# Order of the split products within a k-tile of a two-layer encoder: both wide ones, then both narrow ones

## The chip, the cores and the metric

The kernel runs on one core of one Trainium2 chip. The metric is the device time of one execution in microseconds. Three runs of the kernel before gave 2452.22, 2452.59 and 2452.0 us, median 2452.22.

## The reference

The kernel computes a two-layer encoder trunk over one sequence of 256 tokens with 2048 features, in float32. Each layer is a token mixer and a gated MLP, both behind an RMSNorm and with a residual add:

```python
for layer in range(DEPTH):
    hn = rmsnorm(h, norm_mix_g[layer])
    if layer % 2 == 0:
        mix = mlstm_mixer(hn, ...)      # q, k, v, o, gates = hn @ w_in; two directions; y @ w_out
    else:
        mix = hgrn_mixer(hn, ...)       # q, i, g, f_f, f_b = hn @ w_in; two directions; y @ w_out
    h = h + mix
    h = h + conv_glu(rmsnorm(h, norm_ffn_g[layer]), ...)   # u = hn @ w_up; gelu(conv3(a)) * v; @ w_down
return rmsnorm(h, final_g)
```

D_FF is 5504, so an MLP's up-projection has 2 x 5504 columns. Some 110 million float32 weights are read once, and the work is mainly the products of these weights with 256 tokens.

## The kernel before

**Split products.** To get float32 accuracy from a faster matmul format, both operands are split into a high part (the value rounded to the format) and a low part (the rest). A product x w is taken as three terms: high x high, high x low and low x high. ACT makes the high part of a weight piece (`wh`, L146), DVE the low part (`wl`, L147). Activations are stored as `xt`, `ya`/`yb` or `g` tiles of 128 x 512: columns 0 to 255 hold the high part of 256 tokens, columns 256 to 511 the low part.

**Chunks.** All weights go through one stream of chunks (`stream`). A chunk is a block of output columns, contracted over `nk` k-tiles of 128 rows.

- Feature-major chunks (`fm`, 256 output columns) hold weights stationary: a k-tile is two halves `f` = 0, 1 of 128 columns, each with its own PSUM bank `ps[f]`. For each half L197 sends the whole activation tile through `wh` (512 columns: high and low part), and L198 sends its high part through `wl` (256 columns), adding to the first 256 columns of the same bank. So a k-tile is four matmuls with four different stationary operands.
- Token-major chunks (`tm`, 512 columns) hold activations stationary and send the weights: three products of 512 columns for each of two token blocks (L187 to L189).
- The chunk `first` is token-major with one more 128-column part, and the last chunk of the kernel (`last`, L176) is a feature-major chunk in which all products are 256 columns wide.

Feature-major are: q, k and the output projection of the first mixer; all up- and down-products of both MLPs (43 up-chunks of 16 k-tiles, 8 down-chunks of 22 and 8 of 21 k-tiles per layer); 24 chunks and the output projection of the second mixer.

**Supply.** SP loads raw pieces of 2048 columns into 3 buffers; each gives two `wh` and two `wl` pieces of 1024 columns (4 k-tiles of a feature-major chunk) in 4 buffers each, fetched three pieces ahead. PSUM gives four banks to chunks (`psm`, tag `mm`), so a chunk's two banks are used again two chunks later, and four to everything else (`psa`, tag `aux`).

**Side work.** The heads of both mixers run as generators (`Side`): `side.tick(dt)` behind each k-tile advances a count and emits the next step of any job that is due. The steps' matmuls are `S` (L426), `pn` (L440), `pz` (L468, L691), `pd` (L616, L657, L658) and `py` (L670).

**Order.** The program text gives an order, and the tile framework's scheduler, which works with a model of the engines' times, may move instructions within their dependencies. So the order on PE is that of the built program, not quite that of the loops. When a chunk's last k-tile is sent, `ch.done(ps)` emits its readers: ACT copies the low part out of PSUM (`b`, L209 or L310) and DVE adds (L210, or L311 and L312).

Of the kernel before, what the change touches and what calls it, by code (L numbers as in the profile page):

```python
# [15 lines left out]
P = 128  # L16
T = 256
# [36 lines left out]
def trunk_kernel(ctx, tc, xT, pp_d, cst_d, w_first, w_aq, w_ak, w_av, w_ao, w_aout,  # L54
                 w_bq, w_bv, w_bg, w_bout, w_up, w_down, out, mscr, stop=9):
    nc = tc.nc
    act, dve, pool, pe = nc.scalar, nc.vector, nc.gpsimd, nc.tensor
# [16 lines left out]
    def col(name, i):  # L74
        o = OFF[name] + i
        return pp[:, o:o + 1]
# [5 lines left out]
    class Side:  # L82
        def __init__(self):
            self.now, self.jobs = 0.0, []
# [25 lines left out]
    side = Side()  # L110


    class Chunk:
        def __init__(self, kind, src, nk, x, done, before=None, last=False):
            self.last = last
            self.kind, self.src, self.nk, self.x, self.done, self.before = kind, src, nk, x, done, before
            self.width = {"fm": 256, "tm": 512, "first": 512 + P}[kind]

    def split_weights(chunks):

        first = True
        for ch in chunks:
            total = ch.nk * ch.width
            cuts = [0]
            if ch.last and total % 1024:
                cuts.append(total % 1024)
            if first:
                cuts = [k * ch.width for k in FIRST]
            while cuts[-1] < total:
                cuts.append(min(total, cuts[-1] + 2048))  # L130
            step = ch.width if first else 1024
            for b0, b1 in zip(cuts, cuts[1:]):
                n = b1 - b0
                raw = wpool.tile([P, 2048], F32, tag="raw", bufs=RAW, name="raw")
                nc.sync.dma_start(raw[:, :n], ch.src[:, b0:b0 + n])
                if first:
                    k0, k1 = b0 // ch.width, b1 // ch.width
                    (nc.scalar if k0 < 2 else nc.sync).dma_start(hx[:, k0:k1], xT[:, k0:k1])
                    if k0 == 0:
                        nc.scalar.dma_start(pp[:, 0:KT], pp_d[:, 0:KT])  # L140
                for c0 in range(0, n, step):
                    m = min(step, n - c0)
                    wh = wpool.tile([P, 1024], F32R, tag="wh", bufs=WB, name="wh")
                    wl = wpool.tile([P, 1024], F32R, tag="wl", bufs=WB, name="wl")
                    r = raw[:, c0:c0 + m]
                    act.copy(wh[:, :m], r)  # L146
                    dve.tensor_tensor(wl[:, :m], r, wh[:, :m].bitcast(F32), ALU.subtract)  # L147
                    yield wh, wl, m // ch.width
            first = False

    def stream(chunks):
        pieces = split_weights(chunks)
        ready = []

        def fetch():
            p = next(pieces, None)
            if p is not None:
                ready.append(p)

        for _ in range(LOOK):  # L160
            fetch()
        for ch in chunks:
            if ch.before:
                ch.before()
            ps = [psm.tile([P, 512], F32, tag="mm", name="mm") for _ in range(3 if ch.kind == "first" else 2)]
            k = 0
            while k < ch.nk:
                fetch()
                wh, wl, n = ready.pop(0)
                if ch.last:  # L170
                    for f in range(2):
                        for kk in range(n):
                            x, c = ch.x(k + kk), kk * 256 + f * P
                            terms = ((wh, 0), (wl, 0), (wh, T))
                            for i, (w, o) in enumerate(terms):
                                pe.matmul(ps[f][:, 0:T], w[:, c:c + P], x[:, o:o + T], start=(k + kk == 0 and i == 0),  # L176
                                          stop=(k + kk == ch.nk - 1 and i == 2))
                    k += n
                    continue
                for kk in range(n):  # L180
                    x = ch.x(k)
                    st, sp = k == 0, k == ch.nk - 1
                    if ch.kind != "fm":
                        c = slice(kk * 512, (kk + 1) * 512)
                        for t in range(2):
                            xh, xl = x[:, t * P:(t + 1) * P], x[:, T + t * P:T + (t + 1) * P]
                            pe.matmul(ps[t], xh, wh[:, c], start=st, stop=False)  # L187
                            pe.matmul(ps[t], xh, wl[:, c], start=False, stop=False)  # L188
                            pe.matmul(ps[t], xl, wh[:, c], start=False, stop=sp)  # L189
                        if ch.kind == "first":  # L190
                            pe.matmul(ps[2], wh[:, 512:512 + P], x, start=st, stop=False)
                            pe.matmul(ps[2][:, 0:T], wl[:, 512:512 + P], x[:, 0:T], start=False, stop=sp)
                        side.tick(1.3)
                    else:
                        for f in range(len(ps)):
                            c = kk * ch.width + f * P
                            pe.matmul(ps[f], wh[:, c:c + P], x, start=st, stop=False)  # L197
                            pe.matmul(ps[f][:, 0:T], wl[:, c:c + P], x[:, 0:T], start=False, stop=sp)  # L198
                        side.tick(0.325 * len(ps))
                    k += 1  # L200
            ch.done(ps)

# [9 lines left out]
    def fm_scaled(ps, R, dst, scale=None):  # L212
        fm_sum(ps, dst)
        if scale is None:
            dve.tensor_tensor(dst, dst, R, ALU.mult)
        else:
            dve.scalar_tensor_tensor(dst, dst, scale, R, ALU.mult, ALU.mult)
# [101 lines left out]
    def slot(j, name, more=None):  # L319
        where = keep if j < KT else more  # L320
        return where.tile([P, 2 * T], F32R, tag=f"yt{j}", name=f"{name}{j}")
# [415 lines left out]
    def ffn(layer, norm, nxt):  # L737
        stack = ExitStack()
        box = {}
        chunks = []  # L740

        def begin():
            box["mp"] = stack.enter_context(tc.tile_pool(name="ff", bufs=1))

        def done_up(f, i, GT):
            def go(ps):
                mp, R = box["mp"], norm.R
                a = mp.tile([P, T], F32, tag="a", bufs=2, name="a")
                v = mp.tile([P, T], F32, tag="v", bufs=2, name="v")
                c = mp.tile([P, T], F32, tag="c", bufs=2, name="c")  # L750
                fm_scaled(ps[0], R, a)
                fm_scaled(ps[1], R, v)
                cw = [col("conv_w", (layer * 3 + w) * FT + f) for w in range(3)]
                dve.tensor_scalar(c, a, cw[1], col("conv_b", layer * FT + f), ALU.mult, ALU.add)
                dve.scalar_tensor_tensor(c[:, 1:T], a[:, 0:T - 1], cw[0], c[:, 1:T], ALU.mult, ALU.add)
                dve.scalar_tensor_tensor(c[:, 0:T - 1], a[:, 1:T], cw[2], c[:, 0:T - 1], ALU.mult, ALU.add)
                act.activation(c, c, AF.Gelu)
                dve.tensor_tensor(c, c, v, ALU.mult)
                g = slot(i, "g", mp)
                act.copy(g[:, 0:T], c)  # L760
                dve.tensor_tensor(g[:, T:2 * T], c, g[:, 0:T].bitcast(F32), ALU.subtract)
                GT.append(g)
            return go

        for part, (f0, nf) in enumerate(((0, FA), (FA, FB))):
            GT = []
            for i in range(nf):
                chunks.append(Chunk("fm", w_up[layer, f0 + i], KT, norm.x, done_up(f0 + i, i, GT),
                                    begin if f0 + i == 0 else None))
            chunks += project(lambda c: w_down[layer, c][:, f0 * 256:(f0 + nf) * 256], nf,  # L770
                              lambda k, GT=GT: GT[k], nxt if part else None)
        return chunks, stack.close
# [12 lines left out]
    if stop > 1:  # L785
        c, close0 = ffn(0, n1, n2)
        chunks += c
    if stop > 2:
        c = hgrn(n2, n3)
# [7 lines left out]
    if stop > 3:  # L797
        c, close1 = ffn(1, n3, nf)
        chunks += c
    stream(chunks)  # L800
    side.drain()
    if stop > 3:
# [90 lines left out]
```

## Time and profile before

| | us |
|---|---|
| median of three runs | 2452.22 |
| profiled execution, its own time | 2451.01 |
| its span, first to last instruction | 2449.2 |
| PE busy | 2432.1 |
| PE weight loads (beside PE) | 2108.3 |
| DVE busy | 1759.7 |
| ACT busy | 1221.2 |

| stage | from about, us |
|---|---|
| first mixer (q, k, v, o) | 7 |
| its output projection | 310 |
| first MLP | 400 |
| second mixer | 1116 |
| its output projection | 1626 |
| second MLP | 1719 |
| end of the last product | 2436 |

A matmul's duration in the profile reaches from its start to the modelled end of its pipeline, so successive matmuls overlap, and the time that one takes of PE is read from the distance of the starts. PE, PEld, DVE, ACT, POOL and SP are the tensor engine's matmuls and weight loads, the vector, the scalar, the gpsimd and the sync engine. PEq, PEldq and the like are an engine's queue.

### The profile page before, as it was taken

What the parts mean: (1) busy time and instruction counts of PE and PEld (TensorE: products, weight loads), DVE (VectorE), ACT (ScalarE), POOL (GpSimd) and SP (SyncE); (2) the same over time, 40 slices, a digit from 0 to 9 for tenths busy, and PEclk for the clock granted to TensorE, in tenths of its full rate; (3) what the DMA queues carried; (4) which work ended last, traced back from release to release, by engine and by line L of the source; (5) the groups of instructions that cost most, each with busy time, mean ns of one, the idle gap of its engine ahead of it and who ended that gap; (6) DMA issues with size and microseconds to landing.
All of it is one profiled execution on the core that took longest, in us unless ns stands there. A gap on an engine that the chain in (4) does not pass through costs nothing.

```text
span 2449.2 us, 36986 instructions
## 1 busy us (share of the span) xinstructions
PE 2432.1 (99%) x14462; PEld 2108.3 (86%) x14462; DVE 1759.7 (72%) x2943; ACT 1221.2 (50%) x1890; POOL 267.4 (11%) x325
## 2 busy tenths in 40 slices
PE   9999999999999999999999999999999999999998
PEld 7888888888888888888888888888888888888887
DVE  7766577777656777668888888888777755677754
ACT  6655455444444444445455555545544444444443
POOL 0100032000000000122222222224000000000022
PEclk9999999999999999999999999999999999999999
DMA  7654555555556555555544445445555555555553
GB/s 261 189 179 160 184 187 184 191 191 191 179 189 202 189 189 189 181 183 191 172 160 168 162 165 172 160 156 201 186 191 191 186 189 194 189 189 189 185 190 125
DMA packets 65920, 448.88 MB, mean 183 GB/s; under 512 B 7616, under 2 KB 8256, under 8 KB 15568
## 3 DMA queue, kind: packets, MB, share of 16 engines
q1 hardware_dynamic: 63936, 443.03, 54.2%
q0 software_dynamic: 800, 2.16, 0.6%
q8 instruction: 113, 1.85, 0.3%
q10 hardware_dynamic: 1008, 1.32, 0.2%
q14 instruction: 63, 0.52, 0.1%
HBM read 444.32 MB, written 2.16 MB: 182 GB/s over the span
## 4 chain that ended last, share of the span: by engine, by line
PE 98%; DVE 1%; ACT 0%; issue 0%; DMA 0%; SPq 0%; POOL 0%; DVEq 0%; POOLq 0%
PE mm L197 53%; PE mm L198 26%; PE mm L187 5%; PE mm L189 5%; PE mm L188 5%; PE pd L616 1%; PE pn L440 1%; PE mm L176 1%; PE py L670 1%; DVE wl L147 0%; PE S L426 0%; PE pd L657 0%; DMA raw<-in_w_first 0%; DVE QK L629 0%; PE pz L691 0%
## 5 line engine op out<-in xcount | busy, mean ns | idle before, releaser
L147 DVE TENSOR_TENSOR wl<-raw,wh 128x1024 fp32r<-128x1024 f32 (+1 forms) x864 | 1047.5, 1214 | 546.4 <-ACT wh L146 533.5
L197 PE MATMUL mm<-xt,wh 128*128 128x512 f32 x3776 | 1319.5, 395 | 0.0
L146 ACT CAST wh<-raw 128x1024 fp32r<-128x1024 f32 (+1 forms) x864 | 884.1, 1025 | 833.2 <-PE mm L197 481.5
L198 PE MATMUL mm<-xt,wl 128*128 128x256 f32 x3776 | 1049.9, 278 | 0.0
L197 PEld LDWEIGHTS mm<-xt,wh 128*128 128x128 f32 x3776 | 708.3, 188 | 164.3
L198 PEld LDWEIGHTS mm<-xt,wl 128*128 128x128 f32 x3776 | 710.1, 188 | 0.8
L197 PE MATMUL mm<-g,wh 128*128 128x512 f32 x1334 | 462.6, 394 | 0.0
L198 PE MATMUL mm<-g,wl 128*128 128x256 f32 x1334 | 369.5, 277 | 0.0
L197 PEld LDWEIGHTS mm<-g,wh 128*128 128x128 f32 x1334 | 250.1, 188 | 58.0
L198 PEld LDWEIGHTS mm<-g,wl 128*128 128x128 f32 x1334 | 250.5, 188 | 0.0
L187 PE MATMUL mm<-wh,xt 128*128 128x512 f32 x512 | 201.9, 398 | 3.1 <-ACT xt L204 2.5
L188 PE MATMUL mm<-wl,xt 128*128 128x512 f32 x512 | 201.5, 394 | 0.4 <-DVE wl L147 0.4
L189 PE MATMUL mm<-wh,xt 128*128 128x512 f32 x512 | 200.6, 393 | 0.0
L209 ACT COPY b<-mm 128x256 f32<-128x256 f32 x237 | 87.6, 370 | 172.2 <-PE mm L198 172.2
L243 POOL TENSOR_TENSOR acc<-hx 128x256 f32<-128x256 f32 x4 | 4.8, 1203 | 1238.3 <-DVE hx L312 1238.3
L187 PEld LDWEIGHTS mm<-wh,xt 128*128 128x128 f32 x512 | 95.7, 188 | 23.3 <-ACT xt L204 2.7
L189 PEld LDWEIGHTS mm<-wh,xt 128*128 128x128 f32 x512 | 96.5, 188 | 19.9
L188 PEld LDWEIGHTS mm<-wl,xt 128*128 128x128 f32 x512 | 96.5, 188 | 19.4 <-DVE wl L147 0.8
L197 PE MATMUL mm<-yb,wh 128*128 128x512 f32 x256 | 89.6, 396 | 0.0
L197 PE MATMUL mm<-ya,wh 128*128 128x512 f32 x256 | 89.1, 394 | 0.0
L246 POOL TENSOR_TENSOR sq<-hx 128x256 f32<-128x256 f32 x52 | 62.7, 1214 | 193.4 <-DVE hx L312 191.2
L210 DVE TENSOR_TENSOR a<-mm,b 128x256 f32<-128x256 f32 x86 | 36.5, 425 | 50.9 <-ACT b L209 50.7
(188 smaller groups left out, 1999.2 us busy)
## 6 DMA issues: line engine op xcount, KB each, us to landing
raw<-in_w_up SPq DMA_DIRECT2D x172, 1024.0 KB, 4.9
raw<-in_w_down SPq DMA_DIRECT2D x64, 1024.0 KB, 4.8
raw<-in_w_bq SPq DMA_DIRECT2D x48, 1024.0 KB, 4.9
raw<-in_w_ao SPq DMA_DIRECT2D x16, 1024.0 KB, 4.9
raw<-in_w_aout SPq DMA_DIRECT2D x16, 1024.0 KB, 4.9
raw<-in_w_bv SPq DMA_DIRECT2D x16, 1024.0 KB, 4.9
raw<-in_w_bg SPq DMA_DIRECT2D x16, 1024.0 KB, 4.9
raw<-in_w_bout SPq DMA_DIRECT2D x16, 1024.0 KB, 4.9
```

The source lines that it names most:

```text
L146: act.copy(wh[:, :m], r)
L147: dve.tensor_tensor(wl[:, :m], r, wh[:, :m].bitcast(F32), ALU.subtract)
L176: pe.matmul(ps[f][:, 0:T], w[:, c:c + P], x[:, o:o + T], start=(k + kk == 0 and i == 0), stop=(k + kk == ch.nk - 1 and i == 2))
L187: pe.matmul(ps[t], xh, wh[:, c], start=st, stop=False)
L188: pe.matmul(ps[t], xh, wl[:, c], start=False, stop=False)
L189: pe.matmul(ps[t], xl, wh[:, c], start=False, stop=sp)
L197: pe.matmul(ps[f], wh[:, c:c + P], x, start=st, stop=False)
L198: pe.matmul(ps[f][:, 0:T], wl[:, c:c + P], x[:, 0:T], start=False, stop=sp)
L209: act.copy(b, ps[:, T:2 * T])
L210: dve.tensor_tensor(dst, ps[:, 0:T], b, ALU.add)
L246: eng.tensor_tensor(s, hT[k], hT[k], ALU.mult)
L440: pe.matmul(pn[:, 0:258], w, v, start=(i == 0), stop=(i == len(parts) - 1))
```

## The change

In a feature-major k-tile, the two 512-column products of both halves are sent first and the two 256-column products after them; the call of `side.tick` stands between the two pairs. A chunk that is made with `plain=True` keeps the 512, 256, 512, 256 order, with `side.tick` behind all four. Only the up-products of the first layer's MLP are plain. Token-major chunks and the last chunk are as before. Lines below the edited loop move down by four.

```diff
     class Chunk:
-        def __init__(self, kind, src, nk, x, done, before=None, last=False):
-            self.last = last
+        def __init__(self, kind, src, nk, x, done, before=None, last=False, plain=False):
+            self.last, self.plain = last, plain
...
                     else:
-                        for f in range(len(ps)):
-                            c = kk * ch.width + f * P
-                            pe.matmul(ps[f], wh[:, c:c + P], x, start=st, stop=False)
-                            pe.matmul(ps[f][:, 0:T], wl[:, c:c + P], x[:, 0:T], start=False, stop=sp)
-                        side.tick(0.325 * len(ps))
+                        cs = [slice(kk * ch.width + f * P, kk * ch.width + (f + 1) * P) for f in range(2)]
+                        for f in range(2):
+                            pe.matmul(ps[f], wh[:, cs[f]], x, start=st, stop=False)
+                            if ch.plain:
+                                pe.matmul(ps[f][:, 0:T], wl[:, cs[f]], x[:, 0:T], start=False, stop=sp)
+                        side.tick(0.65)
+                        if not ch.plain:
+                            for f in range(2):
+                                pe.matmul(ps[f][:, 0:T], wl[:, cs[f]], x[:, 0:T], start=False, stop=sp)
                     k += 1
...
                 chunks.append(Chunk("fm", w_up[layer, f0 + i], KT, norm.x, done_up(f0 + i, i, GT),
-                                    begin if f0 + i == 0 else None))
+                                    begin if f0 + i == 0 else None, plain=layer == 0))
```

In the changed file the 512-column product is L197 in both forms; the 256-column product is L199 in a plain chunk and L203 in the others.

## The prediction

> **What bounds the kernel now.** I read the page first, then the waits, then the chain that ended last, in order of time. From the page:
>
> ```profile
> span 2449.2 us, 36986 instructions
> PE 2432.1 (99%) x14462; PEld 2108.3 (86%) x14462; DVE 1759.7 (72%) x2943; ACT 1221.2 (50%) x1890; POOL 267.4 (11%) x325
> PEclk9999999999999999999999999999999999999999
> PE 98%; DVE 1%; ACT 0%; issue 0%; DMA 0%; SPq 0%; POOL 0%; DVEq 0%; POOLq 0%
> L197 PE MATMUL mm<-xt,wh 128*128 128x512 f32 x3776 | 1319.5, 395 | 0.0
> L198 PE MATMUL mm<-xt,wl 128*128 128x256 f32 x3776 | 1049.9, 278 | 0.0
> L198 PEld LDWEIGHTS mm<-xt,wl 128*128 128x128 f32 x3776 | 710.1, 188 | 0.8
> ```
>
> PE carries 98% of the chain at full clock, and the two lines that the change reorders stand with no idle time. A busy PE may still lose time inside its stream, so the waits are not enough; they do say that little is left outside it (engine, line, who was waited for: total us, times, longest):
>
> ```profile
> PE pr L286 <- DVE dg L283: 1.4, 1, 1.4
> ...
> PE pd L616 <- DVE qm L608: 0.8, 1, 0.8
> ...
> PE pd L657 <- DVE QK L630: 0.4, 1, 0.4
> ```
>
> The durations of 395 and 278 ns overlap each other, so they are no price. The price is the step from one start to the next. The chain shows it (start, us taken, what); a row is the time until PE is handed to the next row:
>
> ```profile
> 49.42 0.23 PE mm L197
> 49.65 0.11 PE mm L198
> 49.76 0.23 PE mm L197
> 50.00 0.12 PE mm L198
> 50.11 0.46 PE mm L197 x2
> 50.57 0.24 PE mm L198 x2
> 50.81 0.23 PE mm L197
> ...
> 250.23 0.23 PE mm L187
> 250.45 0.23 PE mm L188
> 250.68 0.23 PE mm L189
> ...
> 2420.72 9.95 PE mm L176 x83
> ```
>
> Five readings. (1) An alternating k-tile (512, 256, 512, 256) runs from 49.42 to 50.11: 0.69 us. (2) The next k-tile was put by the scheduler as 512, 512, 256, 256, the order of the change, and runs from 50.11 to 50.81: 0.70 us, 693 ns start to start before rounding. (3) 512 behind 512, in the token-major chunks, steps 0.227 us in the trace, both where the next product adds to the same bank (L187 to L188) and where it goes to the other one (L189 to L187). (4) 256 behind 256, each with its own weights, steps 9.95/83 = 119.9 ns. (5) A clean stretch of the second layer's feed-forward:
>
> ```profile
> 1800.00:2400.00 600.00, 600.00 (x3464) 524.70 (x3463) 400.83 (x607) 285.84 (x407) 18.95 (x19) 1.00 0.57 190
> ```
>
> 600 us over 3464 matmuls is 173.2 ns each, four of them 692.8 ns. These fit one rule of this trace: 227 ns for a 512-column product and 120 ns for a 256-column one, whatever stands before it. 2 x 227 + 2 x 120 = 694 ns, against 692.8 measured in the alternating order.
>
> **The change, part by part.** The four feature-major groups of L197 have 3776 + 1334 + 256 + 256 = 5622 products, so 2811 k-tiles. The first layer's up-products, 43 chunks of 16, are 688 and keep their order; 2123 k-tiles change. Nothing is added or removed in arithmetic, loads, casts or DMAs.
>
> *Steps in the stream.* Before: two steps 512 to 256 and two 256 to 512. After: one each of 512 to 512, 512 to 256, 256 to 256 and 256 to 512. By the rule above both orders give 2 x 227 + 2 x 120, so 0 ns per k-tile. From the two directly timed k-tiles, (2) less (1) is 0.00 to 0.01 us; start to start, both are 693 ns. I take 0. The bounds come from mixing medians of unlike steps: 512 to 256 takes 233 ns, 256 to 512 115.5 ns on average, 512 to 512 227 ns, 256 to 256 120 ns. Replacing one 512-to-256 step and one 256-to-512 step by 512 to 512 and 256 to 256 gives 227 + 120 - 233 - 115.5 = -1.5 ns, or with 233 in place of 227 +4.5 ns: -3.2 to +9.6 us over 2123 k-tiles. These mix how starts are recorded with what they cost, so zero is the nearer row, because it is the same four instructions in the new order.
>
> *Weight loads.* Each product still has its load, and two loads per k-tile still have only a 256-column product to hide behind. What is new is that the two short ones follow each other. The load's row says 188 ns; if that bound a short product, the pair L203 to L203 would step 188 and not 120 ns, and the sum would be 2123 x 68 = +144 us. The 83 products of L176 are such a stream, each with its load, and step 119.9 ns. So I price it at 0. The Trainium skill (TensorE: Matmul & The Clock Gate, section LDWEIGHTS) gives a load as its columns over 1.2 GHz, so 107 ns for 128 of them: by that figure the load just fits under a 256-column product and this term is 0, where the 188 ns of the profile's row, taken as occupancy, makes it +144 us; the L176 stream agrees with the skill's figure and not with the row read that way.
>
> *Waits.* In the built program the PE queue holds 200 semaphore instructions in place of 56: ahead of L197, 130 of them wait for DVE where 4 did, because the second half's 512 product now comes ahead of the first wait for `wl` that used to cover the release of its PSUM bank. Queued behind such a wait on PE is the whole product stream. The bank was last read two chunks earlier; in the trace the last reader of a feature-major chunk ends at most 7.05 us after that chunk's last product and never less than 4.17 us before the chunk that takes the bank over. The reads of the first half start some 0.23 us later than now, because its 256 product moves behind the other half's 512; 4.17 - 0.23 leaves 3.9 us. So the waits are met when they are reached. The instruction itself:
>
> ```profile
> L197 PEldq EVENT_SEMAPHORE  x9: 51/51/51, 47.1 to 1971.6; - x9
> ```
>
> 144 x 51 ns = 7.3 us if all stood open. Four such stand within 0.4 us ahead of L197 at 652.9 us, and the steps around them stay 0.23 and 0.11 to 0.12 us. I take 0 and keep 7.3.
>
> *Weights and DMAs.* `wh` of a piece comes free some 0.12 us earlier, `wl` unchanged. ACT waits 481.5 us in all for L197 to release `wh`, DVE 533.5 us for ACT, PE 0.4 us once for `wl`; nothing on this path is late, and an earlier release starts casts earlier at no gain. SP's order of transfers is the same.
>
> *Side work.* `side.tick` moves from behind the pair of 256 products to between the 512s and the 256s; per k-tile it counts 0.65 as before. The built order shows where the head work lands: stretches of products are cut 111 times, not 120. One cut, the block at 1230 us: the nine steps ahead of it take 2.04 us, the nine behind 2.08 us, so 0.04 us beside the work itself; over the run the entry and settling come to about 0.1 us per cut. Nine fewer are -0.4 to -0.9 us; I take -0.6. The two waits of PE in the gated layer's start (0.8 and 0.4 us) belong to the second head's block; there DVE has the same 85 instructions to do first, and PE reaches it 0.2 us of products later, so about 1.0 of 1.2 us stays. The transposes of the finished heads stand 1 to 3 us earlier on PE, but their DVE work stands up to 5.5 us earlier too. Bounds: -1.2 (both waits go) to 3 x 1.2 = +3.6 us (the same waits come back in each of the other three groups of four heads).
>
> Sum: 0 + 0 + 0 - 0.6 = -0.6 us against the profiled execution's 2451.0 us (span 2449.2 and 1.8 around it): 2450.4. The median of the runs, 2452.2, lies 1.2 above that execution, so 2451.6.
>
> **The rivals.**
>
> *Banks, faster.* The step 512 to 256 goes to the same bank and takes 233 ns, 6 more than 512 to 512. If that is a wait for the bank just written, the new order, which changes bank at every product, loses it: 2 x 6 x 2123 = -25 us, 2426.6. Against: L187 to L188 stays in one bank and takes 227; 256 to 512 gives the 6 ns back (115.5 against 120). Chance 0.05.
>
> *Two short products in a row, slower.* The second load finds no slack saved up by a long product. From +9.6 us (the +4.5 ns above) up to +144 us (188 ns): 2461 to 2596; it decides from 4.9 us / 2123 = 2.3 ns per k-tile on. For it: a 120 ns step against a 188 ns load. Against: L176 and the k-tile at 50.11 us. Chance 0.04.
>
> *Semaphores, slower.* The 144 extra instructions are not run ahead of the products: +7.3 us, 2458.9; it passes 0.2% once two thirds are open. Against: the four at 652.9 us. Chance 0.04.
>
> *The order is undone.* The scheduler could have put the products back; the built program has 2099 steps 512 to 512 and 2090 steps 256 to 256 in place of 6 and 6, so this is out.
>
> **How the numbers follow.** No change within 0.2% (4.9 us, about what a measurement of this kernel can tell from none): 0.84. Faster: banks 0.05 and 0.02 for a luckier placement of side work, 0.07. Slower: 0.04 + 0.04 and 0.01 for side work, 0.09. The low end takes 1.2 and 0.9 us of side work off 2452.2, and 2 us more for the settling after cuts, which in all costs some 7 us in this trace: 2448. The high end adds the 3.6 us, with a further 1.2 for semaphores that stand open near the cuts: 2457. The rivals beyond hold less than 2 in 10.
>
> **What would show it.** Right: in a clean stretch of the second layer four products still take 693 ns; the chain reads 0.46 and 0.24 for the pairs; L197 and its 256-column partner show no idle time; the waits of PE are the same few. Wrong by banks: a k-tile of about 681 ns, everywhere outside the first layer's up-products. Wrong by loads: a pair of 256 products over 0.24 us. Wrong by semaphores: gaps only at starts of chunks. Wrong by side work: new waits of `pd`, `pz` or `S` for DVE between 20 and 310 us or 1116 and 1640 us.

## The result and the profile after

The changed kernel takes 2462.67 us (median of five runs, 2460.86 to 2462.79) against 2452.22: a ratio of 1.004, 95% interval 1.0028 to 1.0052. It is slower by about 10 us, where no change was forecast. The profiled execution took 2462.67 us with a span of 2460.9 us, 11.7 more than before. Two of the five executions took 2460.86 and 2461.18 us; the step between them and the others, some 1.7 us, is taken up with the waits below.

The page after, the lines that answer to those of before:

```profile
span 2460.9 us, 37193 instructions
PE 2440.9 (99%) x14462; PEld 2116.9 (86%) x14462; DVE 1758.4 (71%) x2943; ACT 1213.6 (49%) x1890; POOL 256.2 (10%) x325
PEclk9999999999999999999999999999999999999999
PE 95%; DVE 3%; issue 1%; ACT 0%; DMA 0%; SPq 0%; POOL 0%; DVEq 0%; POOLq 0%
L197 PE MATMUL mm<-xt,wh 128*128 128x512 f32 x3776 | 1237.4, 396 | 0.0
L203 PE MATMUL mm<-xt,wl 128*128 128x256 f32 x2400 | 478.4, 279 | 0.0
L199 PE MATMUL mm<-xt,wl 128*128 128x256 f32 x1376 | 386.2, 281 | 0.0
```

PE is busy 8.8 us longer with the same 14462 matmuls, and the three groups shown still have no idle time: most of the loss is inside the stream. DVE has a larger part of the chain, 3% for 1%. The waits of PE (engine, line, for whom: total us, times, longest):

```profile
PE pd L661 <- DVE QK L634: 3.1, 5, 0.7
...
PE mm L197 <- DVE hx L315: 1.8, 1, 1.8
```

The first was 0.4 us (and 0.8 us for another tile of the same block), the second was not there.

Where the 11.7 us went, by the starts of the chunks in the two traces: first product 0.35 us earlier; first mixer -1.1; its output projection +0.4; first MLP +5.7, of which its up-products, **whose order was not changed**, +4.5 and its down-products +1.15; second mixer -2.0; its output projection +5.55; second MLP +3.4; the end +0.2.

The same clean stretch as before (busy us and count of each engine; the second number on PE is the matmuls in 600 us), and a part of it in the chain:

```profile
1800.00:2400.00 600.00, 600.00 (x3448) 524.23 (x3447) 397.65 (x607) 280.90 (x405) 15.07 (x15) 1.00 0.57 188
```

```profile
2000.00 0.23 PE mm L203 x2
2000.23 0.47 PE mm L197 x2
2000.70 0.23 PE mm L203 x2
2000.93 0.46 PE mm L197 x2
```

3448 for 3464 products. Start to start, a grouped k-tile takes 696.7 ns on average (696.7 and 696.6 in turn), against 693.3: +3.3 ns, in every clean grouped chunk of this run. The pairs read as the prediction said, 0.46 or 0.47 and 0.23; one k-tile cannot show 3 ns at this resolution, the count over 600 us can.

The surprise is the other clean stretch, of up-products that alternate in both kernels. Kernel before, then after, 200 us in each half of the first layer's up-products:

```profile
430.00:630.00 200.00, 200.00 (x1156) 174.90 (x1156) 146.35 (x235) 98.64 (x145) 0.00 (x0) 1.00 0.57 190
780.00:980.00 200.00, 200.00 (x1156) 174.91 (x1155) 146.30 (x235) 98.60 (x144) 0.00 (x0) 1.00 0.57 190
```

```profile
430.00:630.00 200.00, 200.00 (x1156) 176.67 (x1155) 146.62 (x236) 98.97 (x145) 0.00 (x0) 1.00 0.57 190
780.00:980.00 200.00, 200.00 (x1134) 173.79 (x1133) 143.24 (x232) 97.11 (x141) 0.00 (x0) 1.00 0.56 185
```

The first half is equal, 1156 and 1156. In the second half the same order at the same full clock gives 1134 for 1156. Start to start, a k-tile takes 706.7 ns there, in all 21 chunks, where it takes 693.3 in the first half. So this order has two paces.

### The profile page after: what moved, and what is told of

It reads as the page before. It is cut to its first block, busy times and chain, and to the rows that moved or that the text cites. A ratio compares the mean times of both kernels' runs of the same rounds, so it can differ in the third digit from the quotient of the medians.

```text
span 2460.9 us, 37193 instructions
## 1 busy us (share of the span) xinstructions
PE 2440.9 (99%) x14462; PEld 2116.9 (86%) x14462; DVE 1758.4 (71%) x2943; ACT 1213.6 (49%) x1890; POOL 256.2 (10%) x325
## 4 chain that ended last, share of the span: by engine, by line
PE 95%; DVE 3%; issue 1%; ACT 0%; DMA 0%; SPq 0%; POOL 0%; DVEq 0%; POOLq 0%
PE mm L197 53%; PE mm L203 20%; PE mm L199 7%; PE mm L189 4%; PE mm L188 4%; PE mm L187 4%; DVE wl L147 1%; PE pd L620 1%; PE pn L444 1%; PE mm L176 1%; PE py L674 1%; DVE QK L633 0%; DVE QK L634 0%; DVE qm L612 0%; PE pd L661 0%
## 5 line engine op out<-in xcount | busy, mean ns | idle before, releaser
L197 PE MATMUL mm<-xt,wh 128*128 128x512 f32 x3776 | 1237.4, 396 | 0.0
L197 PEld LDWEIGHTS mm<-xt,wh 128*128 128x128 f32 x3776 | 626.4, 189 | 61.5
L203 PEld LDWEIGHTS mm<-xt,wl 128*128 128x128 f32 x2400 | 450.0, 188 | 102.4
L203 PE MATMUL mm<-xt,wl 128*128 128x256 f32 x2400 | 478.4, 279 | 0.0
L197 PE MATMUL mm<-g,wh 128*128 128x512 f32 x1334 | 419.0, 396 | 0.0
L199 PE MATMUL mm<-xt,wl 128*128 128x256 f32 x1376 | 386.2, 281 | 0.0
L203 PEld LDWEIGHTS mm<-g,wl 128*128 128x128 f32 x1334 | 251.0, 188 | 58.7
L203 PE MATMUL mm<-g,wl 128*128 128x256 f32 x1334 | 262.2, 278 | 0.0
L199 PEld LDWEIGHTS mm<-xt,wl 128*128 128x128 f32 x1376 | 260.3, 189 | 0.1
L197 PEld LDWEIGHTS mm<-g,wh 128*128 128x128 f32 x1334 | 203.4, 189 | 0.1
L213 ACT COPY b<-mm 128x256 f32<-128x256 f32 x237 | 79.7, 368 | 62.4 <-PE mm L199 62.4
L197 PE MATMUL mm<-yb,wh 128*128 128x512 f32 x256 | 83.4, 402 | 1.8 <-DVE hx L315 1.8
L197 PE MATMUL mm<-ya,wh 128*128 128x512 f32 x256 | 80.8, 396 | 0.0
```

Of the source, the lines that this page charges most:

```text
L197: pe.matmul(ps[f], wh[:, cs[f]], x, start=st, stop=False)
L199: pe.matmul(ps[f][:, 0:T], wl[:, cs[f]], x[:, 0:T], start=False, stop=sp)
L203: pe.matmul(ps[f][:, 0:T], wl[:, cs[f]], x[:, 0:T], start=False, stop=sp)
L213: act.copy(b, ps[:, T:2 * T])
```

## The experiments

Two theories were set against each other first. **A:** the grouped order has one pace of 696.7 ns per k-tile, the alternating order has two, 693.3 and 706.7, and keeps the one in which it was started. **B:** the second half of the first layer's up-products is slow by its place or its buffers.

**All up-products grouped too**

```diff
-                                    begin if f0 + i == 0 else None, plain=layer == 0))
+                                    begin if f0 + i == 0 else None, plain=False))
```

> The first layer's up-products are grouped too, so every feature-major k-tile but the last chunk's is 512, 512, 256, 256. Theory A (the grouped order has one pace of 696.7 ns per k-tile, the alternating one has two, 693.3 and 706.7, and keeps the one in which it was started): the up-products of the first layer run at 696.7 ns in both halves; against the changed kernel the second half gains 336 x 10 = 3.4 us, the first half loses 352 x 3.3 = 1.2 us: about 2.2 us less, 2460.4 us or so. Theory B (the second half of these up-products is slow in the changed kernel by its place or its buffers, not by its order): they stay near 706 ns there, and the time rises by 1.2 us.

Measured: 2460.85 us (before 2452.03; ratio 1.0034, interval 1.0022 to 1.0047). The first layer's up-products run at 696.7 ns in both halves, the first MLP is 2.2 us shorter than in the changed kernel. As A said; B would have kept the second half near 706.

**Only the first down-part grouped**

```diff
-        def __init__(..., last=False, plain=False):
+        def __init__(..., last=False, plain=True):
...
+                              plain=not (layer == 0 and part == 0))     # in ffn, for the down-chunks
```

> Only the 8 down-chunks of the first layer's first part are grouped (176 k-tiles), everything else alternates as in the kernel before. Theory A: these 176 run at 696.7 ns, +0.6 us, and the alternating stretch behind them is left in its slow pace of 706.7 ns until something on PE interrupts it, so the 336 k-tiles of up-products behind cost +4.5 us and the 168 of the second down part +2.2 us: 2458 to 2460 us. Theory B: only the 176 k-tiles change, +0.6 us, 2452.8 us, and the up-products behind stay at 693.3 ns.

Measured: 2452.75 us (ratio 1.0002, interval 0.9993 to 1.0011). The 176 k-tiles cost their 0.6 us, and the up-products behind them stayed at 693.3 ns. So part of A falls: coming out of a grouped stretch is not enough to be caught. But the second pace showed up elsewhere: the last chunks of the second mixer's output projection, some 900 us behind the only edit and alternating as before, ran at 706.7 ns per k-tile, and the projection took 1.0 us longer. B's sum of 0.6 us has no such term, so that the median rose by just 0.7 us is in part chance. In 42 us (before, then this kernel):

```profile
1675.00:1717.00 42.00, 42.00 (x245) 36.73 (x244) 30.66 (x38) 21.81 (x31) 18.79 (x16) 1.00 0.56 184
```

```profile
1675.00:1717.00 42.00, 42.00 (x240) 36.44 (x239) 31.11 (x39) 21.56 (x31) 18.56 (x16) 1.00 0.56 187
```

**Only the second MLP grouped**

```diff
-                              lambda k, GT=GT: GT[k], nxt if part else None)
+                              lambda k, GT=GT: GT[k], nxt if part else None,
+                              plain=layer == 0)                         # the rest is plain by default
```

> Only the second layer's MLP is grouped (688 up and 323 down k-tiles); the mixers, both output projections and the first MLP alternate as before. No head work lies there, so this is the price of the order alone: theory A gives 1011 x 3.3 ns = +3.4 us, 2455.6 us, at 696.7 ns per k-tile throughout. If the pace of 696.7 ns came from something else that the change moved (waits on semaphores, side work), the MLP stays at 693.3 ns and the time at 2452.2 us.

Measured: 2455.65 us against 2452.03 (ratio 1.0014, interval 1.0005 to 1.0022); the second MLP is 3.4 us longer by its chunks, all clean ones at 696.7 ns. This is the price of the order alone, free of head work: 1011 k-tiles at 3.33 ns are the whole of it, so nothing is left for the extra semaphore instructions at the chunks' starts. That the median meets the forecast to 0.1 us is in part luck: the profiled execution, 2457.42 us, also has the second mixer's output projection caught at 706.7 ns (+0.9 us) and a first mixer 2.2 us longer, with half clock for 3.4 us from 18.9 us on.

**The tick behind all four products**

```diff
-                        side.tick(0.65)
                         if not ch.plain:
                             for f in range(2):
                                 pe.matmul(ps[f][:, 0:T], wl[:, cs[f]], x[:, 0:T], start=False, stop=sp)
+                        side.tick(0.65)
```

> The changed kernel with side.tick behind all four products, as in the kernel before. If the new waits (PE for DVE: 3.1 us in five blocks of the second mixer's heads, 1.8 us at its output projection, and some 1.7 us of half clock behind that one) come from where the side work is emitted, they go back to 1.2 us and none, and the time falls by 3 to 5.5 us to 2457 to 2460 us. If they come from the order of the products itself (the earlier wait for the PSUM bank), they stay, and the time stays at 2461 to 2463 us.

Measured: 2461.41 us (ratio 1.004, interval 1.0027 to 1.0053). The waits stay, 3.0 us in five and 1.8 us in one. They come with the order of the products and what the scheduler makes of it, not with the place of the tick.

**Three other orders in the second MLP**

```diff
+                if ch.mode:
+                    g = {"turned": 1, "two": 2, "piece": n}[ch.mode]
+                    for k0 in range(0, n, g):
+                        ks = range(k0, min(k0 + g, n))
+                        ...   # the 512-column products of all k-tiles in ks, both halves
+                        ...   # then their 256-column products; "turned": second half first
+                    k += n
+                    continue
```

> Everything alternates as in the kernel before, but the second layer's MLP has three other orders, one in each part: first up-part 'turned' (512, 512, then the 256 of the second half ahead of that of the first, so that the product behind the pair of 512 stays in one bank), first down-part 'two' (four 512 of two k-tiles, then their four 256), second up-part 'piece' (all 512 of a weight piece of up to four k-tiles, then all its 256), second down-part 'turned'. Theory D (what costs is a 256-column product behind a 256-column one, 3.3 ns each): turned 696.7, two 698.3, piece 699.2 ns per k-tile. Theory E (what costs is the passage from a run of wide to a run of narrow products and back, 3.3 ns per passage): turned 696.7, two 695.0, piece 694.2. Theory F (the banks): turned differs from 696.7 and two and piece do not. Time by D 2452 + 4.2 us, by E + 2.0 us.

Measured: 2456.15 us against 2451.87 (ratio 1.0019, interval 1.001 to 1.0028). Per k-tile, start to start: turned 696.7, two 701.7 (two k-tiles take 1401 and 1406 ns in turn), piece 698.3 ns. The chain, of `two` and of `piece`:

```profile
1999.87 0.93 PE mm L187 x4
2000.80 0.48 PE mm L192 x4
```

```profile
2152.53 1.84 PE mm L187 x8
2154.37 0.95 PE mm L192 x8
```

Turned equals grouped, so it is not the banks (F falls). In `piece` eight 256-column products take 0.95 us in the chain, start to start they settle at 120.0 ns, and 512 behind 512 settles at 226.7 ns: short behind short is not what costs (D falls, though its sum of 4.2 us meets the measured 4.3 by accident). The excess lies at the passages: the first five wide products of a run take 27 ns more than 226.7 each would, the first narrow one 7 ns less than 120. So the excess over 693.3 is per passage from a run of wide to a run of narrow products and back, but it is not one price (E falls as it was put): 3.3 ns with runs of two, some 17 ns with runs of four (2 x 8.3), 20 ns with runs of eight (4 x 5.0), and with runs of one 0 or 6.7 ns, by the pace. The Trainium skill (TensorE: Matmul & The Clock Gate, LDWEIGHTS) gives a load's time in ns as its columns over 1.2, an estimate of 107 ns for 128 columns, which would just hide behind a 256-column product; 120 ns per product in the run of eight agrees, though the load's row reads 188 ns.

**Two small products ahead of the slow half**

```diff
+        def kick():
+            t = aux("kick")
+            for _ in range(2):
+                pe.matmul(t[:, 0:P], ones[:, 0:P], ones[:, 0:P], start=True, stop=True)
...
+                                    begin if f0 + i == 0 else kick if layer == 0 and f0 + i == FA else None,
```

> The changed kernel with two small float32 products (128x128, into a spare PSUM bank, read by nobody) on PE ahead of the second half of the first layer's up-products, where the alternating order ran at 706.7 ns per k-tile. Theory A2 (the alternating order has two paces; which one it keeps is settled by the moment at which it starts after a disturbance): the stretch may come out at 693.3 ns, as it did behind the norm's small products at 400 us, and the time falls by 4.5 us less the 0.4 us of the small products, to 2458.5 us; should it stay at 706.7, it is no evidence for another pace but none against either. Theory B (place or buffers): it stays at 706.7 ns, and the time at 2462.9 us.

Measured: 2462.09 us (ratio 1.0042, interval 1.0029 to 1.0054); the stretch stayed at 706.7 ns. This settles nothing by itself, as was said ahead.

**Only the mixers' input projections grouped**

```diff
-            chunks.append(Chunk("fm", w_aq[pr], KT, norm.x, done_q))
+            chunks.append(Chunk("fm", w_aq[pr], KT, norm.x, done_q, plain=False))
...                                   # the same for w_ak and w_bq; plain by default elsewhere
```

> Only the mixers' input projections are grouped (q and k of the first, all 24 chunks of the second: 512 k-tiles); output projections and both MLPs alternate. In the kernel before most of these ran at 706 to 710 ns. Theory A: they come to 696.7 ns, about 3 us less; against it stand the waits that the scheduler's placement brings in the second mixer (3.1 us in place of 1.2). If the MLPs keep 693.3 ns: 2450 to 2452 us; if one of their parts is caught at 706.7 ns, 4 us more each. If grouping costs 3.3 ns everywhere (no second pace): 2452.2 + 1.7 + 1.9 = 2455.8 us.

Measured: 2466.16 us, the slowest of all, against 2451.87 (ratio 1.0059, interval 1.0045 to 1.0072). No MLP product was touched, yet the whole first MLP was caught at 706.7 ns: +13.8 us by its chunks, and +1.5 us in the projection ahead of it. The second mixer's output projection, caught at 706.7 ns in its last chunks, took 2.9 us longer. The second MLP came out at 693.3. The five executions lie between 2465.84 and 2466.52 us, so this is not a chance of one of them.

```profile
430.00:630.00 200.00, 200.00 (x1134) 173.53 (x1133) 143.20 (x229) 96.62 (x142) 0.00 (x0) 1.00 0.56 185
780.00:980.00 200.00, 200.00 (x1134) 173.38 (x1133) 142.34 (x227) 96.84 (x141) 0.00 (x0) 1.00 0.56 186
1800.00:2400.00 600.00, 600.00 (x3463) 524.49 (x3463) 403.70 (x614) 285.74 (x407) 14.98 (x15) 1.00 0.57 190
```

1134 in both halves, where before and after have 1156 in the first: the pace is not tied to a place.

**Only the second mixer grouped**

```diff
+                                    plain=False))                       # for w_bq
...                                   # plain by default elsewhere
-            tail = project(lambda c: w_bout[c], KT, yx, nxt)
+            tail = project(lambda c: w_bout[c], KT, yx, nxt, plain=False)
```

> Only the second mixer is grouped, its output projection too (384 + 128 k-tiles). If the waits (PE for DVE 3.1 us at the heads, 1.8 us at the output projection) come from the placement inside this mixer, they all stand here, and the time is 2452.2 + 3.5 = about 2455.7 us, the sum of the changed kernel's three stages there (605.9 us against 602.4). If they are an echo of what the stages ahead did to the queues, they are gone and the time is near 2450 us.

Measured: 2453.7 us against 2451.87 (ratio 1.0009, interval 1.0 to 1.0018). Both waits stand (3.0 and 1.8 us), so they come from the placement inside this mixer; the mixer is 2.1 us shorter, the output projection 4.0 us longer. It is less than the 3.5 us expected, because that sum held 1.7 us of half clock which this profile lacks. In the run ahead, where `w_bq` was grouped and the output projection alternated, the first wait stood (3.1 us) and the second did not: it belongs to the grouped output projection.

**Only the first mixer grouped**

The edit is that of the mixers run, for `w_aq`, `w_ak` and the output projection `w_aout`.

> Only the first mixer is grouped: q, k and its output projection (128 + 128 k-tiles). By the stages of the changed kernel this is -1.1 us in the mixer (its q and k chunks left the pace of 706 ns) and +0.4 us in the projection. Theory A (the first MLP takes up its pace from what runs ahead of it): its first up-part starts behind a grouped projection and the norm's small products, as in the changed kernel, where it came out at 693.3 ns; then all alternating MLPs stay there and the time is 2452.0 - 0.7 = 2451.3 us. If it is caught at 706.7 ns as in the run with both mixers' input projections grouped, 14 us more, 2465 us. If grouping simply costs 3.3 ns per k-tile against one pace: 2452.9 us.

Measured: 2451.3 us against 2451.86 (ratio 0.9996, interval 0.9987 to 1.0005): as forecast to 0.1 us, but no gain that can be told from none. By chunks -1.0 and +0.4 us; the first MLP is at 693.3 ns throughout. The second mixer's output projection was caught at 706.7 this time and took 0.9 us back, more than the 0.6 won, so the close time is luck; what holds is the pace of the first MLP.

**Nine small products of different lengths**

```diff
+            n = {24: 8, 26: 32, 28: 64, 30: 96, 32: 128, 34: 160, 36: 192, 38: 224, 40: 256}.get(f)
...
+                pe.matmul(t[:, 0:n], ones[:, 0:P], ones[:, 0:n], start=True, stop=True)   # ahead of up-chunk f
```

> The changed kernel with nine small float32 products on PE in the second half of the first layer's up-products, one ahead of every second chunk, of 8, 32, 64, 96, 128, 160, 192, 224 and 256 columns (into a spare bank, read by nobody). The order of the products is untouched. Theory A2 (one order, two paces, and the moment at which the stream starts again decides): the stretch starts at 706.7 ns per k-tile, some of the nine throw it to 693.3 and it keeps this over both chunks until the next one; others leave it or throw it back. Theory B (place or buffers make this stretch slow): all 21 chunks stay near 706.7 ns apart from the small products' own time. Time: 2462 us by B with about 1.5 us of small products; by A2 between 2458 and 2463 us.

Measured: 2464.84 us (two runs; ratio 1.0051, interval 1.0033 to 1.007). The pace at the end of each chunk, start to start: 706.7 ns behind 8, 32, 64, 96 and 128 columns; **693.3 behind 160, kept over both chunks, and behind 192; 706.7 again behind 224 and 256.** The chain around the product of 160 columns shows the turn:

```profile
903.05 0.23 PE mm L197
903.28 0.12 PE mm L199
903.40 0.24 PE mm L197
903.64 0.12 PE mm L199
903.76 0.23 PE mm L197
904.00 0.12 PE mm L199
...
905.88 0.27 PE kick L754 x2
906.16 0.23 PE mm L197
906.38 0.12 PE mm L199
906.50 0.23 PE mm L197
```

Ahead of the small product three pairs take 1.06 us (903.05 to 904.11 in the view, 353 ns each), behind it 0.35 us and less: from 906.50 to 907.89 there are four pairs, 347 ns each. Same code, same place, same clock. A stands in this form: the alternating order has two steady paces, and a small disturbance can throw it from one to the other. B falls. Each length was tried once, in one order and in one profile, so that the length alone decides is not shown. The time lies above both forecasts and settles nothing: the profiled execution, 2466.57 us, has half clock for 3.4 us twice, from 18.6 and from 1663.9 us, and its first mixer alone is 2.5 us longer than the changed kernel's.

## Why the prediction was wrong

The forecast's sum was -0.6 us; the profile shows +11.7. Of these 4.5 are the grouped order's own price, 4.5 the second pace of the up-products that were not edited, and 3.5 a wait and the half clock behind it at the second output projection; the other stages come to -0.8 together. The terms that failed are the steps in the stream and the waits, both taken at 0.

- **The steps in the stream, priced at 0.** The term was mis-sized: +3.3 ns per k-tile, inside the bounds of -1.5 and +4.5 ns. The clean grouped stretches (344 down k-tiles of the first MLP, 1011 of the second) give 1355 x 3.3 = 4.5 us, as their chunks show. I set aside the bound that mixed unlike steps in favour of one k-tile read at 50 us (0.69 and 0.70 us); a 3 ns difference is beyond one row of that view, and one k-tile is not a steady state.
- **"One rule of this trace", with each product's price the same "whatever stands before it".** This step failed outright, and the 0 rested on it. The trace of before held the evidence: around 115 us, in the first mixer, its alternating k-tiles ran at 706.7 ns, three pairs in 1.06 us. The chain there:

```profile
114.83 0.24 PE mm L197
115.07 0.12 PE mm L198
115.19 0.23 PE mm L197
115.43 0.12 PE mm L198
115.54 0.23 PE mm L197
115.77 0.12 PE mm L198
115.89 0.24 PE mm L197
```

  I booked that as settling behind the heads' work (about 7 us over the run). With two paces known, leaving the up-products alone is no guarantee that they keep their time: +4.5 us there. On the other side grouping freed the first mixer from the slow pace, 706 to 696.7 ns, -1.1 us.
- **Waits on the PSUM banks.** The slack of 3.9 us rested on a reading that was wrong. The 4.17 us are those of the first mixer's output projection; at the second's, the trace of before has no slack. Its first chunk's last product ends at 1639.6 us, the first reader of that chunk's banks runs from 1651.35 to 1651.77, and the third chunk's first weight load waits for it:

```profile
1651.35 0.42 DVE L311 TENSOR_TENSOR hx<-hx,mm 128x256 f32<-128x256 f32 x1 [0.63 <-ACT b L310]
1651.82 0.19 PEld L197 LDWEIGHTS mm<-yb,wh 128*128 128x128 f32 x1 [0.19 <-DVE hx L311]
```

  At the same place the changed kernel waits longer, because the scheduler placed DVE's work otherwise. In its chain:

```profile
1655.47 1.06 ACT wh L146
1656.53 0.02 issue
1656.55 0.58 DVE wl L147
1657.13 0.56 issue
1657.69 0.42 DVE hx L315
1658.12 0.04 issue
1658.16 0.50 PE mm L197
...
1659.53 0.43 PE mm L197
```

  The reader of the bank (`hx`, L315) stands in DVE's queue behind a `wl` that waits for a `wh` for which ACT waited on PE. PE loses 1.8 us; 1.1 us after its return the clock is halved for 3.4 us (L197 takes 0.43 for 0.23 us), worth another 1.7 us. The stretch with its granted clock:

```profile
1659.30:1662.70 3.40, 3.40 (x13) 2.91 (x12) 3.40 (x9) 1.67 (x4) 2.35 (x4) 0.50 0.57 171
```

  Six profiles have this wait of 1.8 us: the half clock follows in two (this one and the nine small products), and not in the other four (all up-products grouped, the tick last, two small products, the second mixer alone). That fits the 1.7 us between the five executions: the three of 2462.67 us and more list a mean clock of 0.997, the other two 0.998.
- **Side work.** The bound came nearer than the value: PE now waits in five heads' blocks, 3.1 us for 1.2, about +1.9 where I took -0.6 and kept +3.6. The mixer as a whole is 2.0 us shorter all the same: its chunks run at the better pace, and 40 of the heads' small products moved into the output projection, which holds 92 in place of 52. How much each is worth was not measured apart.
- **The semaphores.** Right at 0: the view of L197 lists 135 of them, 51 ns each, and the second MLP, grouped alone, leaves no time for them.

```profile
L197 PEldq EVENT_SEMAPHORE  x135: 51/51/51, 46.8 to 2326.7; - x135
```

- **The rivals.** None was the cause. "Two short ones in a row" came nearest: 2462.67 us lies in its range of 2461 to 2596, but by accident, since eight of them in a row settle at 120 ns each.

What stays open: why the stream has these paces, and why a passage between wide and narrow products costs 0, 3, 7, 17 or 20 ns by the pattern. The runs show the sizes and that a disturbance can change the pace; they do not show what is in phase with what, nor how an edit changes the pace of a stretch hundreds of microseconds behind it.

## What to carry to other kernels

On a PE that is never idle, price an order by starts over hundreds of products and in every stage, not by one k-tile: here two per cent of a stage lay in steps that one row of a view rounds away. If a stretch that was not edited changes its time, look for a second steady pace before looking for a cause in the edit, and compare the counts of matmuls in equal windows. Read the slack of a buffer at every place where it is used again, since one place without any is enough, and where a scheduler orders the queues do not take the slack of one placement for that of the next.

## What the runs showed of the hardware

- Two steady paces of one instruction sequence at full clock: 693.3 and 706.7 ns per 512, 256, 512, 256 (1.9%), held over hundreds of microseconds; in the profile with nine small products in between, it went from slow to fast behind one of 160 columns and back behind one of 224. The grouped sequence showed one, 696.7 ns.
- In runs of equal products, with a new stationary operand each time, one of 512 columns steps 226.7 ns and one of 256 columns 120.0 ns, start to start: 106.7 ns for 256 columns more, 2.4 columns per ns, and 13.3 ns beside them. The fast alternating pace is the sum, 2 x 226.7 + 2 x 120.0 = 693.4 ns. Other widths were not measured.
- One idle stretch of PE of 1.8 us was followed by 3.4 us at half clock in two of the six profiles that have it. The Trainium skill (TensorE: Matmul & The Clock Gate, "Why this matters for your kernels") warns of idle gaps over some 3 us; here half clock followed a shorter gap, in some executions; that the gap was its cause is likely but was not tested apart.
